# Stores issued from ScalarE and GpSimd instead of SyncE, and the weight remainders of the in-projection on VectorE, in a hybrid encoder block

## The chip, the cores and the metric

The kernel runs on one core of a Trainium2 chip. The metric is the time of one execution on the device in microseconds (us). A core has five engines that each work through a queue of instructions of their own, in order: PE (TensorE, matrix products), DVE (VectorE), ACT (ScalarE), POOL (GpSimd) and SP (SyncE, which only issues transfers). A transfer (DMA) between the main memory (HBM) and the core's own memory (SBUF) is issued as an instruction in the queue of SP, ACT or POOL and then runs by itself on the core's 16 DMA engines; a semaphore tells of its landing. Products go to PSUM, from which ACT or DVE take them.

## What is computed

One layer of an encoder on 2048 tokens of 1024 channels, in float32:

```python
xn = rmsnorm(h, norm_mix_g)
q, k, v, u, y = split(xn @ w_in)            # 512 columns each
q, k = rope(q), rope(k)
attn = dilated_mixture_attention(q, k, v)   # 8 heads of 64, windows with dilation 1, 4, 16
rec = bidirectional_rglru(conv(u), ...) * gelu(y)
h = h + concat(attn, rec) @ w_out
h = h + memory_cross_attention(rmsnorm(h), rmsnorm(mem), ...)
h = h + square(relu(rmsnorm(h) @ w_mlp_in)) @ w_mlp_out
return rmsnorm(h)
```

## The kernel before, in words

**Arithmetic.** Products of float32 matrices are made from split operands: of an operand t, ACT makes h, a rounded copy, and another engine the remainder l = t - h. A product is then three (`mm3`, L120 to L123: h by h, h by l, l by h).

**Order of the work.** The code is written with a framework that records instructions, orders each engine's queue by a planned time and by priority (the order of the code, unless it says otherwise), and puts in all semaphores. So a transfer stands in its issuer's queue where the plan expects it to be ready, and whatever stands behind it in that queue waits with it. `tc.issue_after(ins)` holds instructions of its block, those on the engine of `ins` alone, behind `ins` in the queue.

**Stages.** The in-projection (L212 to L634) takes the columns of `w_in` in ten units of 256, for two blocks B of 1024 tokens each. Weights come through `unit_steps` (L226): four loads of 256 KB a unit into `wraw` (three buffers), h by ACT (L234), l by POOL for the first and DVE for the second load of each half (L235). The kinds of units are u and y (`uy_unit`, L403; result by DVE at L416, for y a GeLU on ACT at L418, stored at L420), q and k (`qk_unit`, L423, with `rope`, L378) and v (`v_unit`, L439; stored at L467). `rope` makes six DVE operations of two products, splits the two results (rh by ACT at L392, rl by DVE at L393, two buffers each), and stores both at L394 and L395, 256 KB a store, to `q_d` or `k_d`; such a store goes to four heads, 32 channels and 512 tokens. Beside the q, k and v units the recurrence runs in pieces (`lru`, L470; its gates' products share PE, its result is stored at L551). The keys and values of the memory (`memory_kv`, L272) are stored at L302, L303 and L311. The 1 / rms of each token is made by POOL (L117, L118), and where it is wanted as a row on all partitions, `rows` (L158) stores it to memory (L160) and loads it back, spread over the partitions (L161).

**The passage to attention** (L628 to L634): while the last k and q units run, `load_head` for head 0 issues queries and keys on POOL (L184, L187) and `near()`, the values of the undilated pattern, on SP (L193 to L195). `far()` (L198 to L202, the other patterns' values) is put behind `last["store"]`, the last rotary store, by `issue_after` (L633). Head 1's loads on POOL are put behind head 0's regrouping of keys (`regroup`, L696, on POOL).

**Attention** (L637 to L888) takes eight heads, three patterns each, in units of two tiles of 128 queries: scores (L750, L751), a masked minimum on DVE (L754), exponentials on ACT (L757), transposes (L766), the split of the weights (L769, L770) and products with the values (L783 to L785). Patterns 1 and 2 are stored to `o_d` (L805, L808) and loaded back in the order of the tokens (L810); `merge` (L817) puts the patterns together on DVE and POOL. Between the units, `rec_half` (L658) makes the recurrent half of the out-projection: a tile xt of x is loaded (L673, two buffers), the product added by DVE (L682) and the sum stored to `hp_d` (L683).

**After it** come the attention half of the out-projection (`half_out`, L905; loads at L935, stores of `h1_d` at L943), the cross-attention (stores of `h2_d` at L1071), and the MLP (from L1244), with its own stores `hid_d` (L1172) and `out` (L1417).

All stores are issued on SP (`dma`, L44). On POOL (`dma_r`, L45) are only the loads of the heads' queries and keys and of the memory's keys and values.

Of the kernel before, what the change touches and what calls it, by code (L numbers as in the profile page):

```python
# [17 lines left out]
S = 2048  # L18
# [21 lines left out]
def hybrid_block(ctx: ExitStack, tc: tile.TileContext, prm, x, xT, mem, memT, pos, masks, w_in, gate_w,  # L40
# [4 lines left out]
    dma_r = nc.gpsimd.dma_start  # L45
    P = 128
# [78 lines left out]
    class RowSum:  # L125
        """sums of squares over the channels of n tokens, and from them 1 / rms on every partition"""
# [31 lines left out]
        def rows(self, dst, line):  # L158
            """by way of memory"""
            dma(ap(line, 0, [[1, P], [P, self.n // P]]), self.r)  # L160
            dma(dst, ap(line, 0, [[0, P], [1, self.n]]))  # L161

        def rows_now(self, dst):
            """by the tensor engine"""
# [13 lines left out]
    def load_head(hd_p, h):  # L178
        """queries [qh; ql], keys [kh; kh] and [kl; kl], values in the groups that the windows take"""
# [32 lines left out]
    # ---------------------------------------------------------------- in-projection  # L212
    psum_phase("psum1", m0=2, m1=2, a=2, b=2)
    sh = ExitStack()
    with ExitStack() as s12:
# [10 lines left out]
        def unit_steps(src, r, sums=None):  # L226
            for kk in range(2):
# [3 lines left out]
                for k in range(0, 4, 2):  # L231
# [3 lines left out]
                    (dve if k else pool).tensor_tensor(l[:, k:k + 2, :], t, f32(h[:, k:k + 2, :]), op=ALU.subtract)  # L235
# [5 lines left out]
        def unit_w(src, lazy=False, sums=None):  # L241
            """256 columns of a weight: for each half of the contraction (h, l) [P, 4, 256]."""
# [29 lines left out]
        def memory_kv(p1):  # L272
# [12 lines left out]
            for c in range(8):  # L285
# [13 lines left out]
                if c < 4:  # L299
                    act.activation(eh, e, AF.Copy)  # L300
                    dve.tensor_tensor(el, e, f32(eh), op=ALU.subtract)
                    dma(km_d[0, :, c, :], f32(eh))  # L302
                    dma(km_d[1, :, c, :], f32(el))  # L303
                else:
# [5 lines left out]
                    for z, tt in ((0, eh), (1, el)):  # L310
                        dma(vm_d[z, :, :, 128 * (c - 4):128 * (c - 4) + 128],  # L311
                            f32(tt).rearrange("p (j d) -> p j d", j=2))

        def x_block(xr_pool, B, wide=2, n_bufs=5, tag="xr", sums=None, with_w=iter(())):
            """1024 tokens of x transposed, times the gain, split: hs[th][k], ls[th][k] of [P, 512]."""
# [24 lines left out]
        def tables(B, load=False):  # L340
            """rows of 1 / rms, and cos and sin times it, of 1024 tokens"""
# [7 lines left out]
        def row_tables(B, th, s, rbn):  # L349
            """1 / rms of 512 tokens: as columns, and as rows"""  # L350
# [27 lines left out]
        def rope(pa, pb, C, Sn, scale, dsts):  # L378
# [10 lines left out]
            for half, src in ((0, t0), (1, t2)):  # L389
# [4 lines left out]
                dma(dsts[half][0], f32(h))  # L394
                last["store"] = dma(dsts[half][1], f32(l)).ins  # L395
# [7 lines left out]
        def uy_unit(W, X, B, n2, kind, rbn, step, sums=None):  # L403
            for th in range(2):
                os = []
                for c in range(2):
# [5 lines left out]
                    while os:  # L412
# [7 lines left out]
                        dma((u_d if kind == "u" else gy_d)[ch, :, t0:t0 + 512], e)  # L420
# [18 lines left out]
        def v_unit(W, X, B, n2, step, sums):  # L439
            # a column of values is divided by the norm of its column of weights (which bounds it), then split in two  # L440
            for th in range(2):
                for m2 in range(2):
# [22 lines left out]
                    for z in range(2):  # L465
                        r = 8 * B + 4 * th + 2 * m2 + z
                        dma(ap(v_d[n2], r * P * VW, [[VW, P], [S * VW, 4], [1, VW]]), vb[:, 4 * z:4 * z + 4, :])  # L467
                    step()

        def lru(lr):  # L470
            """the recurrence, in pieces"""
# [68 lines left out]
            def backward(ct, c):  # L540
# [5 lines left out]
                for z in range(2):  # L546
# [4 lines left out]
                    dma(rec_d[ct, :, 1024 * c + 512 * z:1024 * c + 512 * z + 512], gy)  # L551
# [20 lines left out]
        # units of 256 columns of w_in, with kind and index  # L572
# [63 lines left out]
    # ---------------------------------------------------------------- attention  # L636
    with ExitStack() as s3:  # L637
# [20 lines left out]
        def rec_half(rp):  # L658
            """x + the recurrent half of the out-projection, in pieces"""
# [3 lines left out]
            for t in range(8):  # L663
# [7 lines left out]
                for d2 in range(4):  # L671
# [11 lines left out]
                    dma(hp_d[b, 2 * d2:2 * d2 + 2, :, tk].rearrange("d p n -> p d n"), xt)  # L683
# [4 lines left out]
        def regroup(t, p, half):  # L688
            """keys of this half's residue classes, class after class"""
# [11 lines left out]
        def half_tiles(t, p, half):  # L701
            # query columns, window start, window part used, width, mask, value groups, output column
# [28 lines left out]
        class Unit:  # L731
            """two tiles of 128 queries of one pattern of one head"""
# [67 lines left out]
            def end_pattern(self):  # L800
                t, p, obp = self.t, self.p, self.obp
                if p > 0:
                    od = o_d[t.h][p - 1]
                    if p == 1:
                        dma(ap(od, 0, [[4 * 66, P], [512 * 66, 4], [1, 264]]),  # L805
                            obp.rearrange("p (j q) d -> p j (q d)", q=4))
                    else:
                        dma(ap(od, 0, [[16 * 66, P], [1, 16 * 66]]), obp.rearrange("p r d -> p (r d)"))  # L808
# [5 lines left out]
                if p == (2 if t.h == 0 else 0) and t.h % 2 == 1 and t.h < 7:  # L814
                    dma(ap(at_d, 128 * (t.h // 2), [[384, P], [128 * 384, 16], [1, 128]]), t.at2)
# [749 lines left out]
```

## Time and profile before

| | |
|---|---|
| time, median of 3 runs | 2929.77 us (2928.48 to 2938.83) |
| span of the profiled execution | 2950.7 us, 39906 instructions |
| PE, DVE, ACT, POOL busy | 2599.9, 1996.3, 1287.3, 1254.4 us |
| SP's queue of transfers (q1) | 261712 packets, 342.17 MB, 39.1% of the DMA engines' time |
| POOL's queue of transfers (q0) | 4288 packets, 27.27 MB, 4.1% |

The profiled execution is one run with the hardware profiler on; its span, from the first to the last instruction, is 2950.7 us, 20.9 us above the runs' median, and the durations in this document are its. In the views a line L12 is line 12 of the kernel; `out<-in` are the program's names for tiles; a queue name with a q (SPq, POOLq) is an instruction of the engine's sequencer, such as the issue of a transfer. "Idle before" an instruction is the time for which its engine did nothing, with what ended it.

### The profile page before, as it was taken

How to read it: one execution, taken by the hardware profiler on the slowest of the kernel's cores; microseconds unless marked ns; L12 is line 12 of the kernel's file. 1: busy time of each engine (PE TensorE's matmuls, PEld its weight loads, DVE VectorE, ACT ScalarE, POOL GpSimd, SP SyncE). 2: the span in 40 equal slices, each digit the busy share in tenths (PEclk: the TensorE clock that was granted, in tenths of full speed). 3: DMA queues.
4: the chain of work that ended last, by engine and by line, in shares of the span. 5: the costliest groups of instructions: out<-in, count | busy, mean ns of one | idle time of the engine just before them, and what ended most of it. 6: DMA issues, size and time to landing. Idle time of an engine off the chain costs nothing. (4 is left out here: it accounts for less than half of the span.)

```text
span 2950.7 us, 39906 instructions
## 1 busy us (share of the span) xinstructions
PE 2599.9 (88%) x14074; PEld 2206.6 (75%) x14074; DVE 1996.3 (68%) x3321; ACT 1287.3 (44%) x2356; POOL 1254.4 (43%) x880
## 2 busy tenths in 40 slices
PE   7887677777679989896998799989999999999997
PEld 6776566666679989785887688878887777778776
DVE  6643546765568878633557844474547999999997
ACT  5418254552556656623443333343333333333352
POOL 2221221202235434333114655555655766666652
PEclk9999788889789999897999899999999999999998
DMA  7442334336577866555335433343335222222213
GB/s 191 142 120 89 102 79 134 111 120 147 170 182 189 209 176 171 176 165 125 90 108 168 136 115 107 111 143 108 114 108 203 96 79 78 73 86 80 72 57 114
DMA packets 266199, 371.98 MB, mean 126 GB/s; under 512 B 92944, under 2 KB 139664, under 8 KB 262928
## 3 DMA queue, kind: packets, MB, share of 16 engines
q1 hardware_dynamic: 261712, 342.17, 39.1%
q0 software_dynamic: 4288, 27.27, 4.1%
q8 instruction: 111, 1.82, 0.3%
q14 instruction: 88, 0.72, 0.1%
HBM read 254.72 MB, written 114.65 MB: 125 GB/s over the span
## 5 line engine op out<-in xcount | busy, mean ns | idle before, releaser
L1298 ACT ACTIVATE c<-raw 128x512 fp32r<-128x512 f32 x162 | 102.3, 632 | 271.0 <-PE m L122 147.0
L1149 POOL TENSOR_TENSOR wl<-wr,wh 128x512 fp32r<-128x512 f32 x96 | 144.0, 1500 | 149.2 <-ACT wh L1148 149.2
L1148 ACT ACTIVATE wh<-wr 128x512 fp32r<-128x512 f32 x128 | 80.9, 632 | 288.0 <-PE m L122 147.5
L757 ACT ACTIVATE sm<-sm,obp 128x256 f32<-128x256 f32 (+1 forms) x384 | 161.7, 467 | 46.8 <-DVE obp L754 40.2
L1149 DVE TENSOR_TENSOR wl<-ws,wh 128x512 fp32r<-128x512 f32 x96 | 83.8, 873 | 127.4 <-ACT wh L1148 114.9
L235 POOL TENSOR_TENSOR wl<-wraw,wh 128x512 fp32r<-128x512 f32 x48 | 69.4, 1450 | 234.1 <-ACT wh L234 210.3
L121 PE MATMUL m<-xh,wh 128*128 128x512 f32 x328 | 133.2, 406 | 30.0 <-DVE e L416 15.4
L754 DVE CUSTOM_DVE_ANT_0 sm<-a,msk 128x256 f32<-128x256 f32 (+1 forms) x384 | 131.3, 372 | 31.9 <-PE a L751 28.2
L769 ACT ACTIVATE ph<-b 128x512 f16<-128x512 f32 (+1 forms) x192 | 100.4, 523 | 94.7 <-PE b L766 92.6
L1170 DVE TENSOR_TENSOR c<-m,c 128x512 f32<-128x512 f32 x64 | 44.2, 690 | 139.1 <-PE m L123 137.1
L770 DVE SCALAR_TENSOR_TENSOR pl<-b,ph 128x512 f16<-128x512 f32 (+1 forms) x192 | 114.7, 598 | 26.6 <-ACT ph L769 22.7
L122 PE MATMUL m<-xl,wh 128*128 128x512 f32 x328 | 132.0, 403 | 0.0
L123 PE MATMUL m<-xh,wl 128*128 128x512 f32 x328 | 131.2, 400 | 0.3 <-POOL wl L235 0.3
L766 PE MATMUL b<-prt,sm 128*128 128x128 f32 x640 | 108.2, 284 | 26.0 <-DVE pl L770 17.2
L1299 POOL TENSOR_TENSOR wh<-raw,c 128x512 fp32r<-128x512 f32 x58 | 94.3, 1641 | 77.2 <-ACT c L1298 65.9
L696 POOL TENSOR_SCALAR kc<-kh 128x1024 fp32r<-128x1024 f32 x32 | 68.2, 2132 | 127.9 <-PE a L750 113.3
L750 PE MATMUL a<-kc,qb 128*128 128x256 f32 x256 | 108.8, 426 | 6.1 <-DVE obp L754 6.1
L234 ACT ACTIVATE wh<-wraw 128x512 fp32r<-128x512 f32 x96 | 58.0, 624 | 127.8 <-DMA wraw<-in_w_in 81.1
L1171 DVE SCALAR_TENSOR_TENSOR c<-c 128x512 f32<-128x512 f32 x96 | 112.7, 1174 | 1.0
L1148 ACT ACTIVATE wh<-ws 128x512 fp32r<-128x512 f32 x96 | 60.3, 629 | 109.9 <-PE m L122 105.6
L123 PE MATMUL m<-t3h,wl 128*128 128x512 f32 x276 | 107.6, 390 | 0.0
L1299 POOL TENSOR_TENSOR wl<-raw,c 128x512 fp32r<-128x512 f32 x58 | 92.5, 1612 | 24.9 <-ACT c L1298 24.9
(554 smaller groups left out, 9771.8 us busy)
## 6 DMA issues: line engine op xcount, KB each, us to landing
wr<-in_w_m SPq DMA_DIRECT2D x64, 512.0 KB
hid_d<-c SPq DMA_DIRECT2D x128, 256.0 KB
wraw<-in_w_in SPq DMA_DIRECT2D x80, 256.0 KB
raw<-in_w_m SPq DMA_DIRECT2D x33, 512.0 KB
rawt<-hid_d SPq DMA_DIRECT2D x26, 512.0 KB
t0h<-hid_d SPq DMA_DIRECT2D x26, 512.0 KB
o_d<-obp SPq DMA_DIRECT2D x16, 528.0 KB
obr<-o_d SPq DMA_DIRECT2D x16, 528.0 KB
```

What stands on the lines that cost most here:

```text
L121: pe.matmul(o, ah, bh, start=start, stop=False, **kw)
L122: pe.matmul(o, ah, bl, start=False, stop=False, **kw)
L123: pe.matmul(o, al, bh, start=False, stop=stop, **kw)
L750: pe.matmul(so, q0, kh[:, w0:w0 + 256], start=True, stop=False)
L754: dve.tensor_tensor_reduce(out=sm, in0=sps[:, 256 * z + o0:256 * z + o0 + kw], in1=msk[:, m:m + kw], op0=ALU.add, op1=ALU.min, scale=1.0, ...
L757: exps.append(act.activation(sm, sm, AF.Exp, scale=-1.0, bias=self.obp[:, oc, 65:66]))
L766: pe.transpose(pt[:, c0:c0 + 128], self.sm[:, z, 128 * g:128 * g + 128], idt)
L770: dve.scalar_tensor_tensor(self.pl[:, :w], pt[:, :w], 1024.0, self.ph[:, :w], op0=ALU.mult, op1=ALU.subtract)
L1148: act.activation(h, self.a[n], AF.Copy)
L1149: last[n % 2] = (pool if n % 2 else dve).tensor_tensor(l, self.a[n], f32(h), op=ALU.subtract).ins
L1171: dve.scalar_tensor_tensor(z, z if n < 6 else o, 0.0, z, op0=ALU.max, op1=ALU.mult)
L1299: self.eng[n].tensor_tensor(l[-1], tk, f32(h[-1]), op=ALU.subtract)
```

## The change

Two names for issuing are added, `dma_p` on POOL and `dma_a` on ACT, and stores that went by `dma` on SP go by these. To ACT go the h parts of the rotary results and of the memory's keys and values, `gy_d`, `o_d`, `h1_d` and `h2_d` (136 stores). To POOL go the l parts of the same, `u_d`, `v_d`, `rec_d`, `hp_d`, `at_d` and the rows of 1 / rms (154 stores). `hid_d`, `out` and all loads stay where they are. `last["store"]` is now a store on POOL; the `issue_after` at L633 is unchanged, and `far()` still issues on SP. In `unit_steps` all remainders l are subtracted by DVE. The rest of the diff takes comments out.

```diff
     dma_r = nc.gpsimd.dma_start
+    dma_p, dma_a = nc.gpsimd.dma_start, nc.scalar.dma_start
...
         def rows(self, dst, line):
-            dma(ap(line, 0, [[1, P], [P, self.n // P]]), self.r)
+            dma_p(ap(line, 0, [[1, P], [P, self.n // P]]), self.r)
             dma(dst, ap(line, 0, [[0, P], [1, self.n]]))
...
                     act.activation(h[:, k:k + 2, :], t, AF.Copy)
-                    (dve if k else pool).tensor_tensor(l[:, k:k + 2, :], t, f32(h[:, k:k + 2, :]), op=ALU.subtract)
+                    dve.tensor_tensor(l[:, k:k + 2, :], t, f32(h[:, k:k + 2, :]), op=ALU.subtract)
...
-                    dma(km_d[0, :, c, :], f32(eh))
-                    dma(km_d[1, :, c, :], f32(el))
+                    dma_a(km_d[0, :, c, :], f32(eh))
+                    dma_p(km_d[1, :, c, :], f32(el))
...
-                        dma(vm_d[z, :, :, 128 * (c - 4):128 * (c - 4) + 128],
+                        (dma_p if z else dma_a)(vm_d[z, :, :, 128 * (c - 4):128 * (c - 4) + 128],
...
-                dma(dsts[half][0], f32(h))
-                last["store"] = dma(dsts[half][1], f32(l)).ins
+                dma_a(dsts[half][0], f32(h))
+                last["store"] = dma_p(dsts[half][1], f32(l)).ins
...
-                        dma((u_d if kind == "u" else gy_d)[ch, :, t0:t0 + 512], e)
+                        (dma_p if kind == "u" else dma_a)((u_d if kind == "u" else gy_d)[ch, :, t0:t0 + 512], e)
...
-                        dma(ap(v_d[n2], r * P * VW, [[VW, P], [S * VW, 4], [1, VW]]), vb[:, 4 * z:4 * z + 4, :])
+                        dma_p(ap(v_d[n2], r * P * VW, [[VW, P], [S * VW, 4], [1, VW]]), vb[:, 4 * z:4 * z + 4, :])
...
-                    dma(rec_d[ct, :, 1024 * c + 512 * z:1024 * c + 512 * z + 512], gy)
+                    dma_p(rec_d[ct, :, 1024 * c + 512 * z:1024 * c + 512 * z + 512], gy)
...
-                    dma(hp_d[b, 2 * d2:2 * d2 + 2, :, tk].rearrange("d p n -> p d n"), xt)
+                    dma_p(hp_d[b, 2 * d2:2 * d2 + 2, :, tk].rearrange("d p n -> p d n"), xt)
...
-                        dma(ap(od, 0, [[4 * 66, P], [512 * 66, 4], [1, 264]]),
+                        dma_a(ap(od, 0, [[4 * 66, P], [512 * 66, 4], [1, 264]]),
...
-                        dma(ap(od, 0, [[16 * 66, P], [1, 16 * 66]]), obp.rearrange("p r d -> p (r d)"))
+                        dma_a(ap(od, 0, [[16 * 66, P], [1, 16 * 66]]), obp.rearrange("p r d -> p (r d)"))
...
-                    dma(ap(at_d, 128 * (t.h // 2), [[384, P], [128 * 384, 16], [1, 128]]), t.at2)
+                    dma_p(ap(at_d, 128 * (t.h // 2), [[384, P], [128 * 384, 16], [1, 128]]), t.at2)
...
-                    dma(h1_d[b, dt], rt)
+                    dma_a(h1_d[b, dt], rt)
...
-                dma(h2_d[self.b, dt], ht)
+                dma_a(h2_d[self.b, dt], ht)
```

## The prediction

> **What bounds the kernel now.** I read the page first, then busy time by stage (the stretches below: us from the span's start, length, busy us of PE, weight load, DVE, ACT and POOL, granted clock, DMA share, GB/s), then PE's waits one by one in the timeline.
>
> ```profile
> span 2950.7 us, 39906 instructions
> 0.00:722.00 722.00, 567.89 (x2740) 478.64 (x2740) 413.38 (x557) 353.43 (x529) 141.58 (x140) 0.89 0.45 122
> 722.00:770.00 48.00, 8.40 (x37) 7.75 (x38) 14.87 (x38) 9.95 (x18) 4.43 (x6) 0.54 0.65 169
> 770.00:1260.00 490.00, 437.60 (x4216) 419.75 (x4216) 377.64 (x1263) 299.08 (x733) 200.76 (x136) 0.93 0.70 184
> 1650.00:2951.00 1301.00, 1238.55 (x5450) 1013.98 (x5448) 976.12 (x1102) 477.88 (x751) 780.15 (x466) 0.98 0.31 102
> ```
>
> PE is the bound, and from 1650 on it is busy 95% of the time; no store that moves lies there. What the change can touch is the 154 us that PE idles in the in-projection (up to 722), the 48 us of the passage to attention with 8.4 us of products in them, and the 52 us of idle in attention. The in-projection's idle time is a handful of long waits. These are the ones whose cause I traced to a transfer (start, duration, instruction; in brackets the idle time before it and what ended it):
>
> ```profile
> 363.31 0.80 PE L121 MATMUL a<-uh,gh 128*128 128x512 f32 x1 [11.63 <-ACT tr L518]
> 409.84 0.58 PE L121 MATMUL m<-wh,xh 128*128 128x256 f32 x1 [10.30 <-ACT wh L234]
> 502.46 0.79 PE L121 MATMUL a<-uh,gh 128*128 128x512 f32 x1 [8.88 <-ACT tr L518]
> 527.88 0.79 PE L122 MATMUL a<-ul,gh 128*128 128x512 f32 x1 [10.43 <-DVE ul L500]
> 545.90 0.58 PE L121 MATMUL m<-wh,xh 128*128 128x256 f32 x1 [5.68 <-ACT wh L234]
> 643.25 0.80 PE L121 MATMUL a<-uh,gh 128*128 128x512 f32 x1 [5.81 <-ACT uh L499]
> 654.08 0.80 PE L122 MATMUL a<-ul,gh 128*128 128x512 f32 x1 [7.05 <-DVE ul L500]
> 751.95 0.58 PE L750 MATMUL a<-kh,qb 128*128 128x256 f32 x1 [29.99 <-DVE t L385]
> ```
>
> ACT and DVE end these waits, but they waited themselves: for the rotary stores (L394, L395) to land, since rh and rl have two buffers each, or for loads that share the SP queue with those stores. First the waits on the stores, as the answers on L394 and L395 list them (us, times), then three stretches: only rotary stores in flight; the heads' loads of GpSimd's queue; wide transfers.
>
> ```profile
>   ACT rh L392: 62.1, 10
>   DVE rl L393: 70.2, 14
> 626.00:642.00 16.00, 11.44 (x73) 10.24 (x72) 6.52 (x10) 10.46 (x15) 1.29 (x1) 0.94 0.26 102
> 730.00:740.00 10.00, 0.00 (x0) 0.00 (x0) 0.00 (x0) 0.00 (x0) 0.00 (x0) 0.50 1.15 201
> 1338.00:1342.00 4.00, 0.00 (x0) 0.00 (x0) 1.39 (x2) 1.26 (x2) 1.51 (x2) 0.50 0.98 335
> ```
>
> The rotary stores run at 102 GB/s with 0.26 of the DMA engines' time, against 335 GB/s at 0.98: they use about four engines of sixteen. One store of 262 KB takes 2.6 us, and the four of 512 tokens 10.3 us, in one file. A load in the same queue waits on those four engines:
>
> ```profile
> 349.41 2.31 SPq L233 DMA_DIRECT2D wraw<-in_w_in  x1
> 360.62 0.63 ACT L234 ACTIVATE wh<-wraw 128x512 fp32r<-128x512 f32 x1 [13.44 <-DMA wraw<-in_w_in]
> 405.18 0.33 SPq L233 DMA_DIRECT2D wraw<-in_w_in  x1
> 409.16 0.63 ACT L234 ACTIVATE wh<-wraw 128x512 fp32r<-128x512 f32 x1 [1.05 <-DMA wraw<-in_w_in]
> 513.83 0.33 SPq L324 DMA_DIRECT2D xr<-in_xT  x1
> 521.99 0.72 ACT L329 ACTIVATE xh<-xr,prt 128x512 fp32r<-128x512 f32 x1 [4.62 <-DMA xr<-in_xT]
> 532.95 1.00 SPq L233 DMA_DIRECT2D wraw<-in_w_in  x1
> 545.22 0.63 ACT L234 ACTIVATE wh<-wraw 128x512 fp32r<-128x512 f32 x1 [6.03 <-DMA wraw<-in_w_in]
> ```
>
> The load issued at 405.18 is used 4.0 us later; the others, behind stores, after 11.2, 8.2 and 12.3 us.
>
> **The change part by part.** All sums are made on the profiled execution, whose span of 2950.7 us is 0.7% above the runs' median of 2929.77; I subtract differences from the median without scaling, which errs by less than 1 us.
>
> *Loads freed from the stores.* Each of those loads should come near 4.0 us. The waits at 363.31, 527.88 and 545.90 shrink by 11.2 - 4.0 = 7.2, by 8.2 - 4.0 = 4.2, and by all of 5.7 (the load gains 8.3); the one at 502.46 hangs on another xr load of this kind and is taken at 4.2 too. Together 21.3 us. The bounds are 0, if the three queues merely share the same engines, and 21.3.
>
> *Rotary stores on two queues.* rh goes by ACT's queue, rl by POOL's. The waits at 409.84, 643.25 and 654.08 (23.2 us) each go back to the landing of a store in such a file of 10.3 us. If the halves drain beside each other the file is two deep, not four, and I take half, 11.6 us. Bounds: 0 and 23.2. The Trainium skill, page "DMA: Bandwidth & Descriptors", section "Why a DMA increments its semaphore by 16 and not by 1", says that the number of engines is the largest up to 16 that divides the slowest dimension of both patterns (here the four heads, which the share of 0.26 agrees with), that HWDGE then takes the lowest-numbered ones, and that GpSimd's queue takes consecutive ones from a cursor that moves round. By that rule the rl stores would leave the engines of the rh stores altogether, and this term would be all of 23.2; no run here shows the cursor.
>
> *The passage to attention.* Two rotary splits of the last unit show what PE waits for through 30 us:
>
> ```profile
> 721.01 0.69 DVE L393 SCALAR_TENSOR_TENSOR rl<-t,rh 128x512 fp32r<-128x512 f32 x1 [1.88 <-DMA k_d<-rl]
> 723.78 0.58 POOL L184 DMA_DIRECT2D qb<-q_d  x1
> 750.00 0.69 DVE L393 SCALAR_TENSOR_TENSOR rl<-t,rh 128x512 fp32r<-128x512 f32 x1 [7.98 <-DMA k_d<-rl]
> ```
>
> In between head 1's loads, issued on POOL's queue (second row), fill the engines (share 1.15 at 730), and the SP queue's stores of 2 KB rows get little of them. On POOL's queue the rl stores of 721 stand ahead of those loads and should land in some 5 us (the least landing time of a POOL transfer below is 4.6). Then the next splits run at about 725, the last unit's two first products of 0.7 us behind them, and attention starts at about 727 instead of 752: 25 us. Bounds: 0, if the loads get ahead of the stores in POOL's queue, and 30. The far loads (L634) are ordered behind `last["store"]` by `issue_after`, which binds only work on that store's engine; with the store on POOL the far loads, on SP, are no longer held and come earlier, beside the last rh stores. Their 1.4 MB at the 201 GB/s of the row at 730 are 7 us of the engines; I price them at nothing, since they share no queue with a store, and keep 7 as the bound.
>
> *All three:* 21.3 + 11.6 + 25 = 57.9 us. Not all of it reaches the end: PE takes its products in a written order, and DVE (413 of 722 us) and ACT (353) stand close behind with work of their own. I let two thirds through, 38.6 us. The passage also ran at 0.54 of the clock; its 8.4 us of products at full clock save 4 more. Gain 42.6 us.
>
> *The subtraction moved to DVE.* In the in-projection:
>
> ```profile
> L235 POOL TENSOR_TENSOR wl<-wraw,wh 128x512 fp32r<-128x512 f32 x48 | 69.4, 1450 | 234.1 <-ACT wh L234 210.3 <-PE m L122 22.5 <-DMA wraw<-in_w_in 1.1
> L235 DVE TENSOR_TENSOR wl<-wraw,wh 128x512 fp32r<-128x512 f32 x48 | 39.5, 824 | 67.2 <-ACT wh L234 67.1
> ```
>
> DVE gains 48 x 0.82 = 39.5 us of work, at 57% busy; it delays PE only where a chain on DVE ends the wait, as in three of the eight rows above. I take a fifth, +8 us; the bounds are -30 (each of 48 raw buffers is free 1.45 - 0.82 = 0.6 us sooner, if every load waited for one) and +39.5. What sooner freed buffers give back is why it is a fifth and not three eighths. POOL loses 69.4 us.
>
> *The issues moved.* Durations of an issue (ns, min/median/max) and a POOL transfer's time to landing:
>
> ```profile
> L394 SPq DMA_DIRECT2D k_d<-rh x16: 503/521/886, 344.7 to 723.7; - x16
> L187 POOL DMA_DIRECT2D kh<-k_d x16: 528/547/586, 697.5 to 1103.2; - x16
> DMA to landing us min/median/max: 4.6/7.6/19.9
> ```
>
> ACT gets 56 issues in the in-projection (32 rotary, 16 gy, 8 of the memory): 56 x 0.52 = 29 us at 49% busy, a sixth of it on PE's path, +5 (0 to 29). Behind a waiting store on ACT stand the next split and the gates' tanh; each store waits for ACT's own last result or for one that ACT needs next anyway. The 16 o_d issues fall in attention, where ACT is 61% busy; the 32 h1_d and 32 h2_d ones stand beside the square (L142) of the same tile, for which ACT waits anyway: 0 (0 to 80 x 0.52 = 42). POOL gets 111 issues there: 111 x 0.55 = 61 us for the 69.4 it loses, so 0; if the 32 v_d stores, with four times the pieces, cost four times as much, 53 us more. In attention POOL gets 35 issues, 19 us, at 41% busy: +3 (0 to 19). The 15 row stores go to POOL, where their value is made; store and reload keep their round trip:
>
> ```profile
> 288.28 0.38 SPq L160 DMA_DIRECT2D sv_d<-svc  x1
> 296.90 0.33 SPq L161 DMA_DIRECT2D svr<-sv_d  x1
> ```
>
> 8.6 us from store to reload, nearly all of it landing: 0 (each from -0.4, SP's issue saved, to +7.6, POOL's median landing on top).
>
> *Sum:* -42.6 + 8 + 5 + 3 = -26.6, so 2929.8 - 26.6 = **2903 us**.
>
> **Rivals.** *The queues share the engines anyway: no change.* The 0.26 rows say that engines, not the queue, limit the rotary stores. If three queues take turns on the same four engines, a load still waits its turn and stores land no sooner; only the passage gains. Of its 25 us half comes through, 12.5, against 16 us of costs: 2933 us. The Trainium skill, page "DMA: Bandwidth & Descriptors", section "Issuing engines are not separate DMA queues", says that transfers from all issuers run on the same 16 engines and that a second issuer saves issue time alone; that is this rival. Against it: loads and stores today stand in one file, which the 11.2 and 12.3 us show.
>
> *POOL's order: slower.* In attention hp_d's 32 stores stand in POOL's queue behind the regrouping and the heads' loads, which wait for PE:
>
> ```profile
> SPq L673 <- DMA hp_d<-xt: 62.0, 20, 12.0
> 921.26 0.37 SPq L673 DMA_DIRECT2D xt<-in_xT  x1
> 931.00 0.58 POOL L187 DMA_DIRECT2D kh<-k_d  x1 [10.09 <-PE a L751]
> 935.18 0.68 DVE L682 TENSOR_TENSOR xt<-r,xt 128x512 f32<-128x512 f32 x1
> ```
>
> xt has two buffers; its reload waits for the store, today (first row) and then. Reload to use is 14 us. A store that waits 10.1 us for PE and then lands behind three loads (up to 19.9) is 20 to 25 us late, and the addition at L682 stalls DVE, with scores and splits queued behind it, by 6 to 11. Six heads, perhaps two stores each, 8.5 us: 102 us at worst; I take one stall and a half a head, 76 us, less the 27: 2979 us. It decides from about 14 us of added landing. For it: POOL idles 10.09 us in front of such loads. Against it: the order is planned, and most stores fall elsewhere.
>
> *The change does not do what it says at the passage:* head 1's loads are put ahead of the last rl stores on POOL. Then 25 us stay lost: two thirds of 32.9 is 22, less 16: 2924 us.
>
> **How the numbers follow.** About 0.5% (15 us) is what a measurement of this kernel can tell from no change. Forecast 0.61 (faster; its own range 2860 to 2915), shared engines 0.16 and loads ahead 0.06 (no change), POOL's order 0.17 (slower). Low end: all terms at their upper bound, 21.3 + 23.2 + 30 + 4 = 78.5, and a few us of cost: 2855. High end: half of POOL's price on half the net gain, 2929.8 + 38 - 13 = 2955. Faster 0.61, same 0.22, slower 0.17.
>
> **What would show it.** Right: the waits of ACT rh and DVE rl on stores fall from 62 and 70 us to under half; wraw loads land in about 4 us beside rotary stores; attention's first product stands within 10 us of the last in-projection product; the DMA share passes 0.26 where only rotary stores run. Wrong: DVE rl still waits as long; DVE L682 waits on xt's load; PE waits for wl L235 on DVE; v_d stores hold POOL over 1 us each.

## The result, and the profile after

The changed kernel takes 2943.86 us (median of 15 runs, 2936.73 to 2955.7) against 2928.48 for the kernel before (15 runs, 2907.62 to 2938.83): a ratio of 1.0061, 95% interval 1.0047 to 1.0076. It is slower by 15 us. The forecast was 2903, faster by 27.

The two profiled executions don't show this difference: their spans are 2950.7 and 2951.8 us. The one of the kernel before was an unusual one, above every one of its runs on record. Stages are therefore compared below between kernels whose program is the same up to the place in question. First the changed kernel's stages (same columns as in the prediction):

```profile
0.00:722.00 722.00, 568.60 (x2740) 480.40 (x2740) 424.54 (x618) 348.98 (x527) 142.97 (x197) 0.88 0.43 123
722.00:770.00 48.00, 17.94 (x153) 17.25 (x154) 22.33 (x53) 16.39 (x34) 11.95 (x11) 0.60 0.78 181
770.00:1260.00 490.00, 431.82 (x4083) 413.44 (x4083) 371.71 (x1232) 290.83 (x713) 222.58 (x170) 0.92 0.66 178
```

PE has more done by 770 (17.9 us of products in the passage where there were 8.4), and less between 770 and 1260: of the 10.2 us of products that are won by 770, 5.8 are gone by 1260. Then PE's waits in the timeline; lines are those of the kernel before plus 2.

```profile
389.36 0.58 PE L123 MATMUL m<-wh,xh 128*128 128x256 f32 x1 [13.38 <-ACT wh L236]
502.64 0.79 PE L123 MATMUL a<-uh,gh 128*128 128x512 f32 x1 [11.33 <-ACT uh L501]
638.59 0.79 PE L124 MATMUL a<-ul,gh 128*128 128x512 f32 x1 [6.38 <-DVE ul L502]
730.02 0.55 PE L752 MATMUL a<-kh,qb 128*128 128x256 f32 x1 [21.46 <-DMA kh<-k_d]
755.30 0.58 PE L752 MATMUL a<-kh,qb 128*128 128x256 f32 x1 [17.13 <-DVE obp L756]
1017.73 0.58 PE L124 MATMUL r<-rl,woh 128*128 128x256 f32 x1 [5.70 <-DVE rl L672]
1599.87 0.79 PE L123 MATMUL m<-oh,coh 128*128 128x512 f32 x1 [6.29 <-DVE ht L1071]
```

Of the waits that the prediction listed, those at 363.31 and 545.90 are gone, and those at 502.46 and 527.88 are down to 2.4 and 5.5. The one at 409.84 has grown to 13.4 (first row), those at 643.25 and 654.08 are about as long as they were (5.5 and 6.4), and the product of the second row waits 11.3 us where it waited 1.4. Attention now starts by waiting for its own keys (kh, and 4.9 us more for kl), and two waits are new: at 1017 and at 1599. The waits of ACT for room in rh and of DVE for room in rl (answers on L394 and L395: us, times) come to 74 and 55 us, where they were 62 and 70 and should have fallen to under half:

```profile
  DMA k_d<-rh: 42.7, 9
  DMA q_d<-rh: 31.4, 4
...
  DMA k_d<-rl: 33.6, 6
  DMA q_d<-rl: 21.4, 2
```

### The profile page after: what moved, and what is told of

It reads as the page before. It is cut to its first block, busy times and chain, and to the rows that moved or that the text cites. A ratio compares the mean times of both kernels' runs of the same rounds, so it can differ in the third digit from the quotient of the medians.

```text
span 2951.8 us, 39736 instructions
## 1 busy us (share of the span) xinstructions
PE 2603.5 (88%) x14074; PEld 2210.9 (75%) x14074; DVE 2006.0 (68%) x3369; ACT 1282.8 (43%) x2352; POOL 1291.9 (44%) x986
## 5 line engine op out<-in xcount | busy, mean ns | idle before, releaser
L123 PE MATMUL m<-xh,wh 128*128 128x512 f32 x328 | 133.5, 407 | 28.5 <-DVE e L418 11.6
L768 PEld LDWEIGHTS b<-prt,sm 128*128 128x128 f32 x640 | 78.9, 149 | 36.0 <-ACT sm L759 12.5
L123 PE MATMUL m<-wh,xh 128*128 128x256 f32 x192 | 63.5, 334 | 44.3 <-DVE v L460 24.2
```

What stands on the lines that cost most here:

```text
L123: pe.matmul(o, ah, bh, start=start, stop=False, **kw)
L768: pe.transpose(pt[:, c0:c0 + 128], self.sm[:, z, 128 * g:128 * g + 128], idt)
```

## The experiments

Each was timed in 5 rounds beside the kernel before on one chip, whose median was 2925 to 2928 us in each batch. A cost in us is the ratio less one, times 2926. "In the order before" means that each instruction of an engine is chained behind the one that it follows in the kernel before, and only the moved stores take the place that the scheduler gives them; PE's and DVE's streams are then the same row by row. The expectations repeat some costs up to 2 us off the table's, which go by the ratios. This is the edit that holds the order (the table in it lists the order):

```diff
-        hybrid_block(tc, *args)
+        hybrid_block(tc, *args); _hold(tc, nc)
...
+    ins = list(nc.cur_bb.bb.instructions)
+    for k in np.frombuffer(zlib.decompress(base64.b64decode(_ORDER_HELD)), np.uint16).tolist():
...
+            tc.add_manual_dep(ins[k], ins[prev].name, mybir.DependencyInfo(
+                mybir.DependencyClass.NoSync, mybir.DependencyReason.DATA), reason="order")
```

| kernel | moved | order | ratio, 95% interval | us |
|---|---|---|---|---|
| e1_subtract | subtraction only | free | 1.0001 (0.9984 to 1.0018) | 0 |
| e2_inproj_stores | in-projection's stores | free | 1.0064 (1.0039 to 1.0089) | +19 |
| e3_attn_stores | attention's stores | free | 1.0076 (1.0046 to 1.0107) | +22 |
| e4_tail_stores | stores after attention | free | 1.0034 (1.0016 to 1.0052) | +10 |
| e5_o_act | o_d to ACT | free | 1.0029 (1.0014 to 1.0044) | +8 |
| e6_hp_pool | hp_d, at_d to POOL | free | 1.0079 (1.0058 to 1.0101) | +23 |
| e7_in_act | in-projection, ACT's share | free | 1.0051 (1.003 to 1.0071) | +15 |
| e8_in_pool | in-projection, POOL's share | free | 1.0037 (1.0018 to 1.0057) | +11 |
| f1_stores_old_order | all stores | before | 1.0043 (1.0022 to 1.0064) | +13 |
| f2_old_stores_new_order | subtraction only | after | 1.016 (1.0133 to 1.0187) | +47 |
| f3_in_stores_old_order | in-projection's stores | before | 1.0022 (1.0002 to 1.0043) | +6 |
| f4_attn_stores_old_order | attention's stores | before | 1.0047 (1.0025 to 1.0069) | +14 |
| g1_rotary_act | rotary, both halves to ACT | before | 1.0011 (0.9995 to 1.0028) | +3 |
| g2_in_no_pool_rotary | as f3, rl on ACT, rows on SP | before | 1.0082 (1.006 to 1.0105) | +24 |
| g3_tail_old_order | stores after attention | before | 0.9977 (0.996 to 0.9994) | -7 |
| g4_hp_old_order | hp_d, at_d to POOL | before | 1.007 (1.0051 to 1.0089) | +20 |
| h1_hp_act_old_order | hp_d, at_d to ACT | before | 0.9998 (0.9983 to 1.0012) | -1 |
| h2_tail_and_o_old_order | stores after attention, o_d to ACT | before | 0.9945 (0.9924 to 0.9966) | -16 |

### One part at a time, the order left to the scheduler

```diff
-                    (dve if k else pool).tensor_tensor(l[:, k:k + 2, :], t, f32(h[:, k:k + 2, :]), op=ALU.subtract)
+                    dve.tensor_tensor(l[:, k:k + 2, :], t, f32(h[:, k:k + 2, :]), op=ALU.subtract)
```

> The kernel before with only the subtraction moved: all of the in-projection's weight remainders on VectorE. Theory 1 (the stores eat what they win: what the in-projection's stores gain up to attention is lost again in attention, where the new queues make the loads and stores wait): this part is nearly free, -3 to +4 us. Theory 2 (VectorE is the price: 48 x 0.82 = 39.5 us more work on an engine that ends a third of PE's waits there): +10 to +20 us, about the whole of the change's +15. Theory 3 (the stores of out-projection and cross-attention on ScalarE's queue cost it): 0.

No cost (-5 to +5 us), so theory 2 falls. The 96 subtractions take 0.685 us each on DVE in the median, and 66.7 us in all, where 48 took 39.5 before: 27 us of added work, not another 39.5.

The next three are the change's own lines, by stage: L160 (in-projection's rows), L302 to L311, L394, L395, L420, L467, L551; then L683, L805, L808, L815; then L160 (later rows), L943, L1071. Of each the first lines:

```diff
-                dma(dsts[half][0], f32(h))
-                last["store"] = dma(dsts[half][1], f32(l)).ins
+                dma_a(dsts[half][0], f32(h))
+                last["store"] = dma_p(dsts[half][1], f32(l)).ins
```

> The kernel before with only the in-projection's stores moved (rotary high halves, gated y and half of the memory's keys and values to ScalarE's queue; rotary low halves, u, v, the recurrence, the other half of the memory's and the row sums to GpSimd's). Theory 1: attention's first product comes some 20 us sooner, as in the changed kernel (730.0 against 751.9), but the wait for the heads' keys and for the first exponentials takes most of it back: -10 to +5 us in all. Theory 2: the stores by themselves do gain what was forecast, -20 to -30 us. Theory 3: -20 to -30 us as well.

```diff
-                    dma(hp_d[b, 2 * d2:2 * d2 + 2, :, tk].rearrange("d p n -> p d n"), xt)
+                    dma_p(hp_d[b, 2 * d2:2 * d2 + 2, :, tk].rearrange("d p n -> p d n"), xt)
```

> The kernel before with only attention's stores moved: hp_d and at_d to GpSimd's queue, o_d to ScalarE's. Theory 1: this is the loss, +10 to +25 us, with longer waits of VectorE for the reload of xt (L673) or of the merge for its reload. Theory 2 and theory 3: within 4 us of no change.

```diff
-                    dma(h1_d[b, dt], rt)
+                    dma_a(h1_d[b, dt], rt)
```

> The kernel before with only the stores after attention moved: h1_d and h2_d to ScalarE's queue, the row sums r1_d and r2_d to GpSimd's. Theory 3: +10 to +20 us, 64 issues of 0.52 us on ScalarE and a later row of sums. Theory 1 and theory 2: within 4 us of no change, since the profiled executions of the two kernels take 1746 and 1744 us from attention's last score product to the end.

All three cost: 19, 22 and 10 us, 51 together, where the whole change costs 15 (by the medians) to 18 (by the ratio). No theory had that. Theory 1 missed e2 and e4, theory 3 missed e2 and e3.

The next four halve the parts: o_d's two stores to `dma_a`; hp_d and at_d to `dma_p`; of the in-projection ACT's share, then POOL's share.

```diff
-                        dma(ap(od, 0, [[16 * 66, P], [1, 16 * 66]]), obp.rearrange("p r d -> p (r d)"))
+                        dma_a(ap(od, 0, [[16 * 66, P], [1, 16 * 66]]), obp.rearrange("p r d -> p (r d)"))
```

> The kernel before with only o_d's 16 stores moved to ScalarE's queue. Theory A (in attention it is o_d: the merge of a head's patterns on VectorE, L824, then waits for the reload of o_d, and the score work queued behind it waits too): +12 to +20 us, and L824's waits for obr sum to about 30 us, as in the kernel with all of attention's stores moved (33.7), against 9 and 11 in two kernels that leave attention as it was. Theory B (it is hp_d on GpSimd's queue, the prediction's rival): within 4 us of no change.

```diff
-                    dma(ap(at_d, 128 * (t.h // 2), [[384, P], [128 * 384, 16], [1, 128]]), t.at2)
+                    dma_p(ap(at_d, 128 * (t.h // 2), [[384, P], [128 * 384, 16], [1, 128]]), t.at2)
```

> The kernel before with only hp_d's 32 and at_d's 3 stores moved to GpSimd's queue. Theory A: within 4 us of no change, since VectorE's waits for the reload of xt (L682) come to 3.9 us at most in the changed kernel. Theory B: +12 to +20 us, with L682 waiting several us for xt.

```diff
-                dma(dsts[half][0], f32(h))
+                dma_a(dsts[half][0], f32(h))
```

> The kernel before with only ScalarE's share of the in-projection's stores moved (rotary high halves, gated y, half of the memory's). Theory C (GpSimd's share is what costs: its rotary stores take 10 to 12 us to land, and the first head's loads, in the same queue, come 18 us later): -10 to +3 us here, the first head's loads stay some 25 us ahead of the in-projection's end. Theory D (56 issues of 0.52 us on ScalarE's instruction stream): +8 to +15 us.

```diff
-                last["store"] = dma(dsts[half][1], f32(l)).ins
+                last["store"] = dma_p(dsts[half][1], f32(l)).ins
```

> The kernel before with only GpSimd's share of the in-projection's stores moved (rotary low halves, u, v, the recurrence, half of the memory's, the row sums). Theory C: +12 to +25 us; the first head's key loads are issued after the last rotary stores of the keys, and attention's first product waits for them, not for the rotary work. Theory D: -10 to +5 us.

Again each half costs, 8 to 23 us. Theories A to D are each wrong somewhere. What all these kernels share is that a moved store makes the scheduler write another order for every engine. So the order had to be taken out.

### The order held

```diff
+    dma_p, dma_a = nc.gpsimd.dma_start, nc.scalar.dma_start
...
-        hybrid_block(tc, *args)
+        hybrid_block(tc, *args); _hold(tc, nc)
```

> All of the change's stores in their new queues, the subtraction left as before, and every other instruction of each engine held in the order that it has in the kernel before (TensorE's and VectorE's streams are the same as before, row by row). Seven parts of the change, each alone, cost 9 to 22 us, and all together cost 15, so their costs don't add; each also made the scheduler write another order. Theory O (the order costs, not the queues): -15 to +4 us, with VectorE's waits of the merge (L824) for obr back at 9 to 20 us. Theory Q (the queues cost): +10 to +20 us.

The converse takes the line of e1, leaves the stores on SP and holds the order of the changed kernel:

```diff
-                    (dve if k else pool).tensor_tensor(l[:, k:k + 2, :], t, f32(h[:, k:k + 2, :]), op=ALU.subtract)
+                    dve.tensor_tensor(l[:, k:k + 2, :], t, f32(h[:, k:k + 2, :]), op=ALU.subtract)
...
+        hybrid_block(tc, *args); _hold(tc, nc)
```

> The converse: all stores on SyncE's queue as before, the subtraction on VectorE, and every instruction but the stores held in the order of the changed kernel. Theory O: +10 to +25 us. Theory Q: within 5 us of no change.

Neither theory alone: the queues cost 13 us in the old order (Q), and the new order is bad for the old queues, +47 (O, and more than it said). An order fits the queues that it was planned for. And for the change as a whole the order adds little: 13 us with it held, 15 to 18 with it free. The in-projection's part and attention's part, with the lines of e2 and of e3 and the held order:

```diff
-                last["store"] = dma(dsts[half][1], f32(l)).ins
+                last["store"] = dma_p(dsts[half][1], f32(l)).ins
...
+        hybrid_block(tc, *args); _hold(tc, nc)
```

> Only the in-projection's stores moved (to both queues), every other instruction in the order before. With the order free this was +17 us. Theory O: -15 to +4 us. Theory Q: +12 to +20 us, above all at the passage, where the first head's key loads share GpSimd's queue with the rotary stores.

```diff
-                    dma(hp_d[b, 2 * d2:2 * d2 + 2, :, tk].rearrange("d p n -> p d n"), xt)
+                    dma_p(hp_d[b, 2 * d2:2 * d2 + 2, :, tk].rearrange("d p n -> p d n"), xt)
...
+        hybrid_block(tc, *args); _hold(tc, nc)
```

> Only attention's stores moved (hp_d, at_d to GpSimd's queue, o_d to ScalarE's), every other instruction in the order before. With the order free this was +20 us. Theory O: within 5 us of no change, and the merge's waits at L824 9 to 20 us in sum. Theory Q: +12 to +22 us, and these waits about 30 us.

f3 lies between the theories, f4 at Q's lower end. These two are the best pair of traces in the study: up to attention, f4 is the kernel before, and PE does the same instructions in the same order in both. PE's waits in f4, then in f3:

```profile
353.46 0.80 PE L121 MATMUL a<-uh,gh 128*128 128x512 f32 x1 [10.69 <-ACT tr L518]
400.29 0.58 PE L121 MATMUL m<-wh,xh 128*128 128x256 f32 x1 [10.41 <-ACT wh L234]
467.34 0.50 PE L121 MATMUL a<-uh,gh 128*128 128x512 f32 x1 [1.96 <-ACT ti L521]
490.27 0.80 PE L121 MATMUL a<-uh,gh 128*128 128x512 f32 x1 [9.87 <-ACT tr L518]
504.51 0.50 PE L121 MATMUL a<-uh,gh 128*128 128x512 f32 x1 [1.64 <-ACT uh L499]
515.67 0.79 PE L122 MATMUL a<-ul,gh 128*128 128x512 f32 x1 [10.43 <-DVE ul L500]
533.26 0.58 PE L121 MATMUL m<-wh,xh 128*128 128x256 f32 x1 [5.53 <-ACT wh L234]
629.25 0.80 PE L121 MATMUL a<-uh,gh 128*128 128x512 f32 x1 [5.29 <-ACT uh L499]
640.10 0.80 PE L122 MATMUL a<-ul,gh 128*128 128x512 f32 x1 [7.06 <-DVE ul L500]
736.82 0.58 PE L750 MATMUL a<-kh,qb 128*128 128x256 f32 x1 [28.67 <-DVE t L385]
749.73 0.58 PE L750 MATMUL a<-kh,qb 128*128 128x256 f32 x1 [9.63 <-DVE obp L754]
```

```profile
356.84 0.50 PE L121 MATMUL a<-uh,gh 128*128 128x512 f32 x1 [3.70 <-ACT tr L518]
407.07 0.58 PE L121 MATMUL m<-wh,xh 128*128 128x256 f32 x1 [12.05 <-ACT wh L234]
480.62 0.80 PE L121 MATMUL a<-uh,gh 128*128 128x512 f32 x1 [6.36 <-ACT ti L521]
501.23 0.80 PE L121 MATMUL a<-uh,gh 128*128 128x512 f32 x1 [6.01 <-ACT tr L518]
519.17 0.80 PE L121 MATMUL a<-uh,gh 128*128 128x512 f32 x1 [5.67 <-ACT uh L499]
526.36 0.80 PE L122 MATMUL a<-ul,gh 128*128 128x512 f32 x1 [5.96 <-DVE ul L500]
644.88 0.80 PE L121 MATMUL a<-uh,gh 128*128 128x512 f32 x1 [9.94 <-ACT uh L499]
654.45 0.80 PE L122 MATMUL a<-ul,gh 128*128 128x512 f32 x1 [6.10 <-DVE ul L500]
733.30 0.58 PE L750 MATMUL a<-kh,qb 128*128 128x256 f32 x1 [9.19 <-DVE t L385]
754.76 0.58 PE L750 MATMUL a<-kh,qb 128*128 128x256 f32 x1 [16.70 <-DVE obp L754]
```

Read in pairs (times are f3's), the four waits for loads behind stores shrink by 7.0, 3.9 and 4.5, and the 5.5 at 533 in f4 is gone: 20.9 us. Other waits grow. By 328, before the first rotary store is issued (348.8), f3 is already 10.5 us behind; the largest of these waits, at 148 and 208, grew by 2.7 each. At 208 DVE waits for a row of 1 / rms, whose store and reload take 9.9 us where they took 8.8. Later those at 407, 480, 519 and 645 grow by 1.6, 4.4, 4.0 and 4.7, and three more, at 438, 543 and 628, by 2.6 to 2.8; the one at 654 shrinks by 1.0. So the in-projection ends at 724.1 instead of 708.1. Then the passage takes 9.2 instead of 28.7, and the first wait behind it 16.7 instead of 9.6. In all f3 is 5.0 us behind at that place, and 6 us in its time.

Behind the waits at 407, 480 and 645 stand rotary stores: ACT or DVE waits for one to land (in front of 480, ACT waits 6.6 us for room in rh, 3.4 in f4). Behind those at 519 and 543 stand loads again, of x and of weights, which are in flight beside rotary stores. This is the time from issue to landing of the rl stores on POOL's queue in f3 (answer on L395), of 256 KB each; in the kernel before, four such stores in one file would take 10.3 us at its 102 GB/s:

```profile
DMA to landing us min/median/max: 6.3/10.8/15.5
```

On ACT's queue (q10 in the views) an rh store gets less while other transfers run. First 472 to 476 us of f3, where SP's transfers (q1) are in flight too, then 484 to 486, where the rh store has the engines almost to itself (packets, MB, share of the 16 engines):

```profile
q1 hardware_dynamic: 176, 0.33, 74.7%
q10 hardware_dynamic: 89, 0.18, 17.7%
```

```profile
q10 hardware_dynamic: 101, 0.20, 26.0%
```

0.18 MB in 4 us are 45 GB/s, 0.20 MB in 2 us are 100.

### What GpSimd's queue costs

```diff
-                dma(dsts[half][0], f32(h))
-                last["store"] = dma(dsts[half][1], f32(l)).ins
+                dma_a(dsts[half][0], f32(h))
+                last["store"] = dma_a(dsts[half][1], f32(l)).ins
```

> Only the rotary stores moved, both halves to ScalarE's queue; every other instruction in the order before. Theory G (what took the gain back is GpSimd's queue): the loads are freed as in the kernel with all of the in-projection's stores moved (20.9 us), and nothing of its losses comes back: -10 to -25 us. Theory D (64 issues of 0.52 us, 33 us of ScalarE): -5 to +10 us.

Beside f3 the next one differs by these lines:

```diff
-                last["store"] = dma_p(dsts[half][1], f32(l)).ins
+                last["store"] = dma_a(dsts[half][1], f32(l)).ins
...
-            (dma if 'r' in banks else dma_p)(ap(line, 0, [[1, P], [P, self.n // P]]), self.r)
+            dma(ap(line, 0, [[1, P], [P, self.n // P]]), self.r)
```

> All of the in-projection's stores moved, but the rotary low halves go to ScalarE's queue too and the row sums stay on SyncE's; the rest as in the change; every other instruction in the order before. Beside the kernel with the in-projection's stores moved in the old order (+5 us), theory G expects the waits that grew there to fall back: those on the row sums (148, 208, 328 us: 2.7, 2.7, 1.9) and those on rotary low halves (481, 519, 645 us: 4.4, 4.0, 4.7), together 20 us: -5 to -20 us in all. Theory D: +5 to +15 us.

Theory G falls: g1 gains nothing, and g2 is worse than f3 by 18 us. Three waits that the theory named did fall in g2 (at 208, 480 and 519 by 2.8, 6.0 and 5.4), but others grew. Its passage takes 36.7 us, and that of g1 30.1: on ACT's queue the last rl stores run beside the heads' loads, and on POOL's (f3, 9.2) ahead of them. POOL's queue, on which rl lands late in the in-projection, is the right one at the passage.

```diff
-                    dma(h1_d[b, dt], rt)
+                    dma_a(h1_d[b, dt], rt)
...
+        hybrid_block(tc, *args); _hold(tc, nc)
```

> Only the stores after attention moved (h1_d, h2_d to ScalarE's queue, r1_d, r2_d to GpSimd's), every other instruction in the order before. With the order free this was +9 us. Theory O (order): -3 to +4 us. Theory Q (queues): +6 to +12 us.

```diff
-                    dma(hp_d[b, 2 * d2:2 * d2 + 2, :, tk].rearrange("d p n -> p d n"), xt)
+                    dma_p(hp_d[b, 2 * d2:2 * d2 + 2, :, tk].rearrange("d p n -> p d n"), xt)
...
+        hybrid_block(tc, *args); _hold(tc, nc)
```

> Only hp_d's and at_d's stores moved to GpSimd's queue, every other instruction in the order before. With the order free this was +22 us. Theory O: within 5 us of no change. Theory B (the prediction's rival: a store behind work and loads in GpSimd's queue delays the reload of xt): +10 to +22 us, with waits for xt at L682.

The stores after attention gain 7 us with the order held, which neither theory had, and cost 10 with it free: there the order is all of the cost. For hp_d it is the queue, +20 against +23. That is theory B, the prediction's rival, by its size; the waits for xt at L682 that it named are absent in g4. Two waits carry most of the difference of e4 and g3, 5.3 and 6.8 us. PE in e4, then in g3 (which has no wait at the second place; the kernel before has 12.9 at the first and none at the second):

```profile
1315.85 0.37 PE L151 MATMUL a<-ones,ss 128*128 128x1 f32 x1 [12.17 <-POOL ss L144]
1573.37 0.80 PE L121 MATMUL m<-oh,coh 128*128 128x512 f32 x1 [6.78 <-DVE ht L1069]
```

```profile
1311.31 0.37 PE L151 MATMUL a<-ones,ss 128*128 128x1 f32 x1 [6.89 <-POOL ss L144]
```

The changed kernel has the second one too (6.29 at 1599.87). The cause of both stands in SP's queue. First e4 (first and second place), then g3 (second place), then the changed kernel, and below it the store of its row of 1 / rms on POOL:

```profile
1307.30 0.32 SPq L161 DMA_DIRECT2D rb<-r_d  x1
1307.75 0.35 SPq L935 DMA_DIRECT2D h<-hp_d  x1
```

```profile
1529.95 27.32 SPq L1065 DMA_DIRECT2D ht<-h_d  x7
1566.94 0.32 SPq L161 DMA_DIRECT2D rb<-r_d  x1
1567.38 8.43 SPq L1065 DMA_DIRECT2D ht<-h_d  x4
```

```profile
1533.13 33.55 SPq L1065 DMA_DIRECT2D ht<-h_d  x10
1579.59 8.00 SPq L161 DMA_DIRECT2D rb<-r_d  x2
```

```profile
1594.23 0.32 SPq L163 DMA_DIRECT2D rb<-r_d  x1
```

```profile
1584.47 0.83 POOL L162 DMA_DIRECT2D r_d<-rr  x1 [0.29 <-POOL rr L120]
```

The reload of the row (rb) stands on SP and waits 9.7 us, from 1584.5 to 1594.2, for POOL's store. The new order puts loads behind that reload (in e4 one of h at the first place and four of ht at the second), so they wait with it; in g3 all eight of h and ten of ht stand ahead of it.

```diff
-                    dma(hp_d[b, 2 * d2:2 * d2 + 2, :, tk].rearrange("d p n -> p d n"), xt)
+                    dma_a(hp_d[b, 2 * d2:2 * d2 + 2, :, tk].rearrange("d p n -> p d n"), xt)
```

> The stores of hp_d and at_d on ScalarE's queue instead of GpSimd's, every other instruction in the order before. If GpSimd's lateness is the cost: -5 to +6 us. If the loss comes from taking the store out of SyncE's stream, whoever issues it: +15 to +25 us, as with GpSimd's queue (+20). Neither theory counts what ScalarE loses where its stream now waits for VectorE's sum: 0 to +8 us on top.

On ACT's queue the same stores cost nothing (-5 to +4 us): it is GpSimd's queue. SP's longer waits for hp_d at L673 (62.0 us before, 145.7 in the changed kernel, 163.0 in g4) are not the cost by themselves: h1 has 126.8 of them. Where g4 loses its 20 us is only partly settled. One place is: DVE's subtraction at L670 takes 8.59 us instead of 1.22 beside POOL's copies and issues, and PE waits 5.6 us for it at 1005. The changed kernel's new wait at 1017 is the same one (8.83 us, PE waits 5.7). The rest can't be assigned. The merge's waits for obr are 24.3 us in g4 and 11.1 in g3, but they differ by 10 us between executions of one program (20.0 in the kernel before, 9.3 in e4, which is the same up to there), and h1, which costs nothing, has 31.2. In the same way g4's profile takes 12 us longer than that of the kernel before between the same two products of PE (at 820 and 1280 us there), but h1's takes 14 longer, and e4's, with the same program, 11 less.

```diff
-                        dma(ap(od, 0, [[16 * 66, P], [1, 16 * 66]]), obp.rearrange("p r d -> p (r d)"))
+                        dma_a(ap(od, 0, [[16 * 66, P], [1, 16 * 66]]), obp.rearrange("p r d -> p (r d)"))
...
-                    dma(h1_d[b, dt], rt)
+                    dma_a(h1_d[b, dt], rt)
...
+        hybrid_block(tc, *args); _hold(tc, nc)
```

> The stores after attention (h1_d, h2_d on ScalarE's queue, r1_d, r2_d on GpSimd's) and o_d's on ScalarE's, every other instruction in the order before. If the parts add with the order held: -7 for the stores after attention, and for o_d the difference between all of attention's stores (+14) and hp_d and at_d alone (+20), -7: -8 to -16 us together, faster than both kernels. If they don't add: -7 to +8 us, with the merge's waits for obr at 25 us or more.

h2 takes 2910.71 us (2901.74 to 2922.0) and beats both kernels. With the order held the parts add, as far as intervals of some 6 us either way can tell: 6 + 14 - 7 = 13 for f3, f4 and g3, and f1 has 13; o_d's part is f4 less g4, -7, and with g3's -7 makes -14, where h2 has -16.

## Why the prediction was wrong, step by step

With the order held, and the subtraction at 0, the in-projection with the passage was forecast at -30 us (-42.6 + 8 + 5) and came to +6, attention was forecast at +3 and came to +14, and the stores after it at 0 and came to -7. So 36 of the 40 us by which the sum is off lie in the first.

*Loads freed from the stores* (21.3 us): right for the four waits that it named, 20.9 us in f3. But two other waits for loads, at 519 and 543, grew by 4.0 and 2.7, beside stores in flight.

*Rotary stores on two queues* (11.6): wrong, and with the sign reversed. The step that failed is "if the halves drain beside each other the file is two deep, not four". Its three waits (409.84, 643.25 and 654.08 before) changed by +1.6, +4.7 and -1.0 from f4 to f3, 5.3 us longer in sum, and one rl store on POOL lands in 10.8 us in the median. The halves do drain beside each other, as the queues' shares of the engines show in the changed kernel where rotary stores of both queues run (q0 is POOL's queue, q10 ACT's, q1 one load of SP's; 376 to 384 us):

```profile
q0 software_dynamic: 522, 0.52, 28.7%
q1 hardware_dynamic: 142, 0.52, 16.3%
q10 hardware_dynamic: 159, 0.31, 12.3%
```

More engines at work did not bring the landing forward: DVE's waits for room in rl fell from 68 to 42 us in f3, ACT's for room in rh rose from 60 to 68, and a store on ACT's queue got 45 GB/s beside SP's transfers where it gets 100 alone. The Trainium skill, page "DMA: Bandwidth & Descriptors", section "Why a DMA increments its semaphore by 16 and not by 1", has GpSimd's queue take consecutive engines from a cursor that moves round, by which the prediction put this term at 23.2 at most. A share of 0.41 for the rotary stores, where one queue had 0.26, agrees with other engines; but a cursor that moves round comes to the rh stores' engines too, and the term is below 0 all the same.

*The passage* (25): right in f3, 19.5 us of it, and by the mechanism that was named: head 1's loads are issued at 752.9, behind the last rl stores at 744.3. But it only makes up for the 16.0 us lost before it, and 8.6 us of it go into the two waits right behind. The "some 5 us" for the landing of these stores were too few: 10.8 in f3's median, up to 23.5 in the changed kernel. There the passage came to 8.5 (21.46 where there were 29.99), because head 0's loads are not where they were. POOL's timeline in the changed kernel, then in e4, whose in-projection is that of the kernel before:

```profile
700.41 1.43 POOL L397 DMA_DIRECT2D k_d<-rl  x2
702.45 1.09 POOL L189 DMA_DIRECT2D kh<-k_d  x2
```

```profile
684.29 1.09 POOL L187 DMA_DIRECT2D kh<-k_d  x2
```

The prediction asked whether head 1's loads would stand ahead of the stores. It didn't ask what the stores do to head 0's loads, which now follow rec_d's and rl's in the same queue, 18 us later. Hence the waits for kh and kl. The far loads (0, at most 7) came sooner, as it said: from 699.8 to 711.9 us, where they stood from 762.3 to 765.4; no run separates what that costs. The 17.1 us behind the keys, where there were 9.7, are another thing again. DVE, then POOL in the changed kernel:

```profile
745.66 8.90 DVE L672 TENSOR_TENSOR rl<-rt,rh 128x1024 fp32r<-128x1024 f32 x1 [1.06 <-ACT rh L671]
```

```profile
745.61 2.00 POOL L698 TENSOR_SCALAR kc<-kh 128x1024 fp32r<-128x1024 f32 x1
```

The regrouping of the late keys, four copies from 745.61 to 753.47, now falls on a DVE operation that the first scores wait behind, and that takes 8.90 us instead of 1.22. In f3, where the keys are late too, it takes 8.95.

*Two thirds come through*: nothing did. In f3 the four waits' 20.9 us are more than lost at 724 us, to waits before and between them. The rival "the queues share the engines" had 0 from both terms, and the 45 GB/s against 100 speak for its mechanism; against it, the four loads did come sooner.

*The subtraction* (+8): 0. *ACT's issues* (+5): not separated; g1, with 64 of them, is at +3 (-1 to +8). *POOL's issues* (0 and +3): 0.75 us each for v_d and 0.76 for hp_d, not 0.55; what their length costs by itself isn't separated either.

*hp_d on POOL* (in the sum at 0, as a rival at 76 us with a chance of 0.17): of the single parts this is the largest loss, 20 us, and none on ACT's queue. The rival had the queue right and its price four times too high, and the stall that it named, L682 waiting for xt, is 3.9 us in one wait of the changed kernel and nothing in g4. Of the 20 us the 5.6 at 1005 are shown; the cause of the rest stays open.

*Row stores* (0, "store and reload keep their round trip"): the round trip nearly stayed, 9.9 us in f3 against 8.8 in f4 at the wait at 208, and that wait grew by 2.7; in g2, with the row stores back on SP, it is 3.1, as in f4 (3.2). What failed is that nothing was named behind the reload. Once the store is on another queue the reload waits on SP, with the loads that the new order put behind it: in e4 this makes two waits longer than in g3, by 5.3 and 6.8 us.

*What the prediction didn't have at all* is that the order is written anew. One part at a time, free and held differ by 12 us for the in-projection, 8 for attention and 17 for the stores after it, all to the bad. It took the order of the kernel before as given and changed queues in it. For the change as a whole this is the smaller matter: 13 of its 15 to 18 us are there with the order held.

## What to carry to other kernels

When a store leaves the queue in which its reload stands, ask what is queued behind that reload, and what is queued behind the store in its new queue; several of the waits that could be traced here stood in those two lists. Where a scheduler writes the order, a change of queue is two changes: hold the order to measure the one. Here the parts added with it held and didn't with it free. A store moved off a load's queue still shares the engines with that load. A forecast gain on a wait counts only as far as the next wait behind it allows, so align two traces of one order and read them in pairs.

## What the runs showed of the hardware

A DVE subtraction of 128x1024 with both inputs in SBUF, 1.22 us in the median of g4, took 8.90 us in the changed kernel when it began beside four copies of POOL back to back; it ended 1.1 us after the last. The Trainium skill, page "SBUF — State Buffer", section "SBUF: two separate sides", says that DVE with two SBUF inputs and a GpSimd operation that reads SBUF take a pair of ports by an exclusive lock, and that the later one is blocked for the whole instruction. The trace agrees with the lock; but DVE sat out four instructions, not one, and in g4 (8.59 us) three copies and the issues of two transfers between and before them.
